# Down projections of a two-layer decoder trunk: seven half-size products for three of four k-tile batches, and a new order of the up and down groups

## The chip, the cores and the metric

The kernel runs on one core of one Trainium2 chip. The metric is the device time of one execution, in microseconds (us), of which the median of several runs is taken. TensorE (PE) multiplies, with its weight loads (PEld) beside it; VectorE (DVE) and ScalarE (ACT) do the elementwise work, GpSimd (POOL) very little of it, and SyncE (SP) issues the loads of the weights.

## What is computed

256 tokens of width 2048 pass through two layers. Each layer adds a mixer (differential attention in the first, an RG-LRU block in the second), a squared-ReLU MLP with 8192 hidden columns, and a gated per-layer embedding:

```python
def sqrelu_mlp(xn, w_up, w_down):
    return jnp.square(jax.nn.relu(xn @ w_up)) @ w_down

    for i in range(DEPTH):                      # DEPTH = 2
        h = h + mix(rmsnorm(h, g_mix[i]))       # attention or RG-LRU
        h = h + sqrelu_mlp(rmsnorm(h, g_mlp[i]), w_up[i], w_down[i])
        ple_gate = jax.nn.sigmoid(rmsnorm(h, g_ple[i]) @ w_ple_gate[i])
        h = h + ple_gate * (p[i] @ w_ple_proj[i])
```

Everything is float32. `w_up` is 2048 x 8192 and `w_down` 8192 x 2048 in each layer.

## The kernel before

All products with weights run through one stream (`stream`). Its unit is a `Group`: 256 tokens by 512 columns of one weight, over `nk` k-tiles of 128 rows. The weights of a group come in chunks of four k-tiles (one load of 1 MB, issued by SyncE at L351, three raw buffers `w_raw`), and each chunk is cut into two `Sub`s of two k-tiles. A sub is split into two float32r parts of 12 significant bits each: ScalarE casts `w_hi` (L255) and VectorE subtracts to get `w_lo` (L256), both 128x1024. Four buffer pairs hold such parts; a sub is split three subs ahead of its products, as far as these buffers allow.

A product of two split operands takes three matmuls per k-tile and token tile (`mm3`, L249 to L251: high by high, low by high, high by low), each of 512 moving columns. One sub of an ordinary group is therefore 2 token tiles x 2 k-tiles x 3 = 12 matmuls. The up projection is computed transposed (`flip`): the weights are the stationary operand and the activations with both parts side by side the moving one, which takes 16 matmuls per sub (L391), 8 of 512 and 8 of 256 columns, on four PSUM accumulators.

The MLP (`mlp`) works in slices of 1024 hidden columns. `up(c)` is two flipped groups over 16 k-tiles, 8 subs each. Their evict (`up_evict`) adds the two halves of each accumulator (ScalarE copy L644, VectorE add L645), takes `relu(.) ** 2` in one VectorE operation (L646) and splits the result into the slice's tiles `big`. `down(c)` is four groups (512 output columns each) over the slice's 8 k-tiles, 4 subs each, and their evict adds the product, scaled by a row factor, to the residual `h` (L589). The slices are emitted as up(0), up(1), down(0), up(2), down(1), and so on, so that two up groups and four down groups alternate.

A scheduler fixes the order of each engine's instructions when the program is built. On the chip each engine then runs its own list in that order, and semaphores make it wait for the others. PSUM has six accumulators `acc` and two tiles `tp`, which serve transposes.

## Time and profile before

| | us |
|---|---|
| median of 3 runs | 2327.42 (2326.64 to 2328.0) |
| profiled execution, span | 2326.8 |
| TensorE busy | 2308.8 (99%) |
| VectorE busy | 1424.6 (61%) |
| ScalarE busy | 1193.6 (51%) |
| the two MLP stages | 707.6 each (403.73 to 1111.34, 1515.47 to 2223.08) |

The span runs from the first to the last instruction of one profiled execution, and lies 0.6 us under the median. Busy time is the union of an engine's instructions. Matmuls are listed with a duration that overlaps the next one, so the pace of TensorE is read from the distance between starts. "Idle before" an instruction is put down to what released it last.

### The profile page before, as it was taken

The numbers are of one execution on the slowest core, as the hardware profiler recorded it, in microseconds if no ns is written. First come the engines' busy times: TensorE is split into PE (matmuls) and PEld (weight loads), VectorE is DVE, ScalarE is ACT, GpSimd is POOL, SyncE is SP. The second block draws the span as 40 slices with busy tenths as digits, with TensorE's granted clock in tenths as the row PEclk, the third lists the DMA queues.
The fourth block names the chain that finished last, engine by engine and source line by source line (L and its number), as shares of the span: only waits on it lengthen the run. The fifth ranks groups of instructions, "written<-read, shape, count | busy, mean of one in ns | idle before, by whom it ended". The sixth has DMA issues, their size and how long they took to land.

```text
span 2326.8 us, 28564 instructions
## 1 busy us (share of the span) xinstructions
PE 2308.8 (99%) x11467; PEld 1946.9 (84%) x11467; DVE 1424.6 (61%) x1704; ACT 1193.6 (51%) x1594; POOL 44.7 (2%) x79
## 2 busy tenths in 40 slices
PE   8999999999999999999999999999999999999999
PEld 6888888888888888888888887888888888888887
DVE  6676655565565665566566767566565555565654
ACT  6555554444444444444558887454444444444453
POOL 2100000000000000000000000000000000000000
PEclk9999999999999999999999999999999999999999
DMA  7454555555565655655566565556565565555554
GB/s 241 163 185 163 165 179 181 185 195 189 191 197 184 198 188 192 196 185 181 189 193 219 187 212 181 181 182 198 184 197 190 191 197 184 198 189 191 177 199 148
DMA packets 225396, 438.95 MB, mean 189 GB/s; under 512 B 7582, under 2 KB 16416, under 8 KB 225264
## 3 DMA queue, kind: packets, MB, share of 16 engines
q1 hardware_dynamic: 224608, 436.24, 57.3%
q8 instruction: 89, 1.46, 0.3%
q0 software_dynamic: 608, 0.89, 0.2%
q14 instruction: 43, 0.35, 0.0%
q10 hardware_dynamic: 48, 0.02, 0.0%
HBM read 435.01 MB, written 2.10 MB: 188 GB/s over the span
## 4 chain that ended last, share of the span: by engine, by line
PE 94%; DVE 2%; ACT 2%; DMA 1%; issue 1%; SPq 0%; POOL 0%; DVEq 0%; ACTq 0%
PE acc L391 31%; PE acc L251 21%; PE acc L249 20%; PE acc L250 20%; PE tp L317 1%; DVE w_lo L256 1%; ACT w_hi L255 1%; DMA w_raw<-in_w_gate_x_dram 0%; DVE t L770 0%; DMA h<-in_x_dram 0%; PE tp L458 0%; DVE big L827 0%; ACT L810 0%; SPq L351 0%; ACT L788 0%
## 5 line engine op out<-in xcount | busy, mean ns | idle before, releaser
L256 DVE TENSOR_TENSOR w_lo<-w_raw,w_hi 128x1024 fp32r<-128x1024 f32 x808 | 987.4, 1224 | 781.4 <-ACT w_hi L255 779.9
L255 ACT CAST w_hi<-w_raw 128x1024 fp32r<-128x1024 f32 x808 | 849.0, 1052 | 979.8 <-PE acc L251 605.7
L391 PE MATMUL acc<-x,w_hi 128*128 128x512 f32 x2048 | 704.8, 394 | 0.0
L391 PE MATMUL acc<-x,w_lo 128*128 128x256 f32 x2048 | 547.8, 278 | 0.0
L249 PE MATMUL acc<-w_hi,x 128*128 128x512 f32 x1152 | 457.1, 397 | 0.0
L250 PE MATMUL acc<-w_lo,x 128*128 128x512 f32 x1152 | 450.2, 391 | 1.9 <-DVE w_lo L256 1.8
L251 PE MATMUL acc<-w_hi,x 128*128 128x512 f32 x1152 | 450.5, 391 | 0.0
L391 PEld LDWEIGHTS acc<-x,w_hi 128*128 128x128 f32 x2048 | 376.0, 188 | 78.6
L249 PE MATMUL acc<-w_hi,big 128*128 128x512 f32 x1024 | 399.7, 390 | 0.0
L251 PE MATMUL acc<-w_hi,big 128*128 128x512 f32 x1024 | 398.6, 389 | 0.0
L250 PE MATMUL acc<-w_lo,big 128*128 128x512 f32 x1024 | 398.4, 389 | 0.0
L391 PEld LDWEIGHTS acc<-x,w_lo 128*128 128x128 f32 x2048 | 384.7, 188 | 11.2
L251 PEld LDWEIGHTS acc<-w_hi,x 128*128 128x128 f32 x1152 | 216.8, 188 | 46.8 <-DVE x L256 0.2
L250 PEld LDWEIGHTS acc<-w_lo,x 128*128 128x128 f32 x1152 | 217.2, 189 | 45.0 <-DVE w_lo L256 3.0
L249 PEld LDWEIGHTS acc<-w_hi,x 128*128 128x128 f32 x1152 | 216.8, 188 | 41.7
L251 PEld LDWEIGHTS acc<-w_hi,big 128*128 128x128 f32 x1024 | 192.2, 188 | 40.3
L250 PEld LDWEIGHTS acc<-w_lo,big 128*128 128x128 f32 x1024 | 192.3, 188 | 39.8
L249 PEld LDWEIGHTS acc<-w_hi,big 128*128 128x128 f32 x1024 | 192.2, 188 | 39.0
L589 DVE SCALAR_TENSOR_TENSOR h<-acc,n_r,h 128x512 f32<-128x512 f32 x128 | 89.9, 744 | 0.0
L644 ACT COPY t<-acc 128x256 f32<-128x256 f32 x128 | 47.5, 371 | 22.8 <-PE acc L391 20.6
L259 ACT ACTIVATE x<-tp,cols_a 128x256 fp32r<-128x256 f32 (+1 forms) x72 | 35.7, 496 | 39.5 <-DVE x L260 39.5
L260 DVE SCALAR_TENSOR_TENSOR x<-tp,cols_a,x 128x256 fp32r<-128x256 f32 (+1 forms) x72 | 36.8, 511 | 18.8 <-ACT x L259 18.8
(173 smaller groups left out, 1064.2 us busy)
## 6 DMA issues: line engine op xcount, KB each, us to landing
w_raw<-in_w_up_dram SPq DMA_DIRECT2D x128, 1024.0 KB, 5.2
w_raw<-in_w_down_dram SPq DMA_DIRECT2D x128, 1024.0 KB, 5.1
w_raw<-in_w_qkv_dram SPq DMA_DIRECT2D x47, 1024.0 KB, 5.2
w_raw<-in_w_ple_gate_dram SPq DMA_DIRECT2D x32, 1024.0 KB, 5.2
w_raw<-in_w_in_rec_dram SPq DMA_DIRECT2D x32, 1024.0 KB, 5.5
w_raw<-in_w_o_attn_dram SPq DMA_DIRECT2D x16, 1024.0 KB, 5.2
w_raw<-in_w_o_rec_dram SPq DMA_DIRECT2D x16, 1024.0 KB, 5.1
w_raw<-in_w_ple_proj_dram SPq DMA_DIRECT2D x8, 512.0 KB, 3.7
```

What stands on the lines that cost most here:

```text
L249: nc.tensor.matmul(ps, lhsT=lh, rhs=rh, start=start, stop=False)
L250: nc.tensor.matmul(ps, lhsT=lh, rhs=rl, start=False, stop=False)
L251: nc.tensor.matmul(ps, lhsT=ll, rhs=rh, start=False, stop=stop)
L255: nc.scalar.copy(hi, src)
L256: nc.vector.tensor_tensor(lo, src, hi.bitcast(F32), op=ALU.subtract)
L259: nc.scalar.activation(hi, src, AF.Copy, scale=scale)
L260: nc.vector.scalar_tensor_tensor(lo, in0=src, scalar=scale, in1=hi.bitcast(F32), op0=ALU.mult, op1=ALU.subtract)
L317: nc.tensor.transpose(tp[:, i, t * P : (t + 1) * P], h[:, t, (k0 + i) * P : (k0 + i + 1) * P], ident)
L391: nc.tensor.matmul(o, lhsT=lh, rhs=rh, start=k == 0 and n == 0, stop=k == g.nk - 1 and n == 1)
L589: nc.vector.scalar_tensor_tensor(hb, in0=acc[t], scalar=scale()[:, t : t + 1], in1=hb, op0=ALU.mult, op1=ALU.add)
L644: nc.scalar.copy(other, ps[:, SEQ:])
```

## The change

The hidden columns of a layer are taken in 16 batches of 4 k-tiles. For three of four batches (those whose number is not a multiple of 4) the down projection is computed on 2 x 2 blocks: token tile by k-tile parity on the left, k-tile parity by 512 output columns on the right. Seven products of such blocks stand in place of eight (`FORMS`), and some of their operands are sums of blocks. The left sums (`S1` to `S4`) are formed in `up_evict`, before the split, so that a hidden tile has eight forms of which seven are used; the right sums (`U1`, `T2`, `T4`, `T3`) are formed on VectorE from the raw weights, each one form ahead of its split (`split_form`).

A `SevenGroup` covers 256 tokens and 1024 output columns (a `half`) over four batches: the three seven batches first, then the plain one. It accumulates in six `acc` tiles and both `tp` tiles. When the products P1, P5, P6 and P7 are complete, `middle` combines them in two `t4` tiles; at the end `evict` adds four accumulators and four combinations to `h`. Per layer the order is up(0), up(1), then the columns 1024 to 2047 of batches 0 and 1 as two plain groups, then seven times two up groups and one `SevenGroup` (half 0 over batches 0 to 3, half 1 over 2 to 5, half 0 over 4 to 7, and so on), and at the end two plain groups over batches 14 and 15. An up group is one batch, 512 hidden columns.

Chunks and split parts of the seven groups may also use one buffer borrowed from `big` and one pair from `v4` (`ring`). `relu(.) ** 2` is now two ScalarE operations (L803, L804). A chunk that appears again within two chunks is no longer loaded again, which concerns the gate weights of the second layer's mixer. Comments and docstrings are gone as well. The core of the diff:

```diff
+X11, X21, X12, X22, S3, S1, S2, S4 = range(8)
+FORMS = (
+    ("W11", X11, "P1"), ("W21", X12, "P2"), ("U1", S1, "P5"), ("T2", S2, "P6"), ("T4", X22, "P4"),
+    ("T3", S3, "P7"), ("W22", S4, "P3"),
+)
+SUMS = {"U1": ("W11", "W12"), "T2": ("U1", "W22"), "T4": ("T2", "W21"), "T3": ("W12", "W22")}
+BT = 4
...
+    def products(self, i, s):
+
+        b, form, nj = self.what[i]
+        x, out = self.hid[b], []
+        if nj is None:
+            _, f, k = FORMS[form]
+            for j in range(2):
+                out.append((k,) + x.form(j, f) + (s.hi[:, j], s.lo[:, j]))
+        else:
+            n, j = nj
+            for t in range(NT):
+                for kk in range(SK):
+                    out.append((self.plain(n)[t],) + x.lhs(2 * j + kk, t) + (s.hi[:, kk], s.lo[:, kk]))
...
-            if not chunks or chunks[-1] is not s.chunk:
+            if not any(c is s.chunk for c in chunks[-2:]):
                 chunks.append(s.chunk)
...
+                turn["raw"] += c.ring
+                if c.ring and turn["raw"] % (W_RAW + 1) == 0:
+                    c.raw = big([P, KC, NB])
+                else:
+                    c.raw = wraw.tile([P, KC, NB], F32, name="w_raw")
...
+        def split_form(s):
+
+            bl = s.blocks
+            src = bl.of(FORMS[s.form][0])
+            nc.scalar.copy(s.hi, src)
+            after = FORMS[s.form + 1][0] if s.form + 1 < len(FORMS) else None
+            if after in SUMS:
+                load_to(cidx[id(bl.chunks[1])])
+                one, two = (bl.of(nm) for nm in SUMS[after])
+                bl.sums[after] = t4([P, SK, NB])
+                nc.vector.tensor_tensor(bl.sums[after], one, two, op=ALU.add)
+            nc.vector.tensor_tensor(s.lo, src, s.hi.bitcast(F32), op=ALU.subtract)
...
+                    turn["split"] += s.chunk.ring
+                    if s.chunk.ring and turn["split"] % (W_SPLIT + 1) == 0:
+                        s.hi, s.lo = (v4([P, SK, NB], F32R) for _ in range(2))
...
+                    for k, lh, ll, rh, rl, first, last in prods:
+                        nc.tensor.matmul(acc[k], lhsT=lh, rhs=rh, start=first, stop=False)
+                        nc.tensor.matmul(acc[k], lhsT=ll, rhs=rh, start=False, stop=False)
+                    for k, lh, ll, rh, rl, first, last in prods:
+                        nc.tensor.matmul(acc[k], lhsT=lh, rhs=rl, start=False, stop=last)
+                    if i == g.mid:
+                        g.middle(acc)
...
-                    nc.vector.scalar_tensor_tensor(u, in0=u, scalar=0.0, in1=u, op0=ALU.max, op1=ALU.mult)
-                    ks = slice(half * 4 + 2 * b, half * 4 + 2 * b + 2)
-                    split(hid[c].hi[:, ks], hid[c].lo[:, ks], u)
+                    nc.scalar.activation(u, u, AF.Relu)
+                    nc.scalar.activation(u, u, AF.Square)
+                    if bt.seven:
+                        nc.vector.tensor_tensor(f[:, S3 : S1 + 1], f[:, X11 : X21 + 1], f[:, X21 : X22 + 1 : 2], op=ALU.subtract)
+                        nc.vector.tensor_tensor(f[:, S2], f[:, S1], f[:, X11], op=ALU.subtract)
+                        nc.vector.tensor_tensor(f[:, S4], f[:, X12], f[:, S2], op=ALU.add)
+                    split(bt.hi[:, j], bt.lo[:, j], f)
...
+            def middle(acc):
+                c1, cb = t4([P, 2, NB]), t4([P, 2, NB])
+                keep["P1"], keep["M"], keep["B"], keep["N"] = c1[:, 0], c1[:, 1], cb[:, 0], cb[:, 1]
+                nc.scalar.copy(keep["P1"], acc["P1"])
+                nc.vector.tensor_tensor(keep["M"], acc["P6"], keep["P1"], op=ALU.add)
+                nc.vector.tensor_tensor(keep["B"], acc["P7"], keep["M"], op=ALU.add)
+                nc.vector.tensor_tensor(keep["M"], acc["P5"], keep["M"], op=ALU.subtract)
+                nc.vector.tensor_tensor(keep["N"], acc["P5"], keep["B"], op=ALU.subtract)
...
-        up(0)
-        for c in range(1, NFC):
-            up(c)
-            down(c - 1)
-        down(NFC - 1)
+        for b in range(0, NBT, 2):
+            up(b)
+            up(b + 1)
+            if b == 0:
+                down_plain(0, 2, None)
+            elif b % 4 == 0:
+                down(1, range(b - 2, b + 2))
+            else:
+                down(0, range(b - 2, b + 2))
+        down_plain(NBT - 2, 2, norm_out)
```

What this does to the engines' lists is seen at three places. The first is VectorE at the end of an up group. Before, the list has the four adds (L645), the two squares (L646) and the splits of the hidden tiles (`big`) among the weight splits (`w_lo`) of the down group that follows:

```order
L645 TENSOR_TENSOR t_8257<-acc,t_8258 128x256
L645 TENSOR_TENSOR t_8257<-acc,t_8261 128x256
L645 TENSOR_TENSOR t_8267<-acc,t_8268 128x256
L646 SCALAR_TENSOR_TENSOR t_8257<-t_8257 128x512
L645 TENSOR_TENSOR t_8267<-acc,t_8271 128x256
L256 TENSOR_TENSOR w_lo<-w_raw,w_hi 128x1024
L256 TENSOR_TENSOR big<-t_8257,big 128x512
L646 SCALAR_TENSOR_TENSOR t_8267<-t_8267 128x512
L256 TENSOR_TENSOR w_lo<-w_raw,w_hi 128x1024
L256 TENSOR_TENSOR big<-t_8267,big 128x512
L256 TENSOR_TENSOR w_lo<-w_raw,w_hi 128x1024 x2
```

Now, at the same place ahead of the first `SevenGroup` (`t_7321` and `t_7335` are the hidden tiles with their forms, `t_7300` is the sum T2, `t_7354` T4, `t_7367` T3, and `v_7365` the low part of T4):

```order
L471 TENSOR_TENSOR w_lo<-t_7300,w_hi 128x1024
L806 TENSOR_TENSOR t_7321<-t_7321 128x256
L807 TENSOR_TENSOR t_7321<-t_7321 128x128
L806 TENSOR_TENSOR t_7335<-t_7335 128x256
L808 TENSOR_TENSOR t_7321<-t_7321 128x128
L807 TENSOR_TENSOR t_7335<-t_7335 128x128
L808 TENSOR_TENSOR t_7335<-t_7335 128x128
L357 TENSOR_TENSOR big<-t_7321,big 128x1024
L357 TENSOR_TENSOR big<-t_7335,big 128x1024
L470 TENSOR_TENSOR t_7354<-t_7300,w_raw 128x1024
L470 TENSOR_TENSOR t_7367<-w_raw 128x1024
L471 TENSOR_TENSOR v_7365<-t_7354,v_7364 128x1024
```

The split of the fourth form stands ahead of the hidden tiles' sums and splits, and the sum T4 for the fifth form behind them; the low parts of the first three forms stand in front of the piece, before the adds L802.

The second place is VectorE inside the groups with `w_down`. Before, four weight splits and two updates of `h` alternate through a whole stretch of four down groups:

```order
L256 TENSOR_TENSOR w_lo<-w_raw,w_hi 128x1024 x2
L589 SCALAR_TENSOR_TENSOR h<-acc,n_r_3441,h 128x512 x2
L256 TENSOR_TENSOR w_lo<-w_raw,w_hi 128x1024 x4
L589 SCALAR_TENSOR_TENSOR h<-acc,n_r_3441,h 128x512 x2
L256 TENSOR_TENSOR w_lo<-w_raw,w_hi 128x1024 x4
```

Now, in the third seven batch of the first `SevenGroup` (`t_7499`, `t_7511`, `t_7525` and `t_7537` are the sums U1, T2, T4 and T3, `v_7549` the low part of T3 and the last split of the batch):

```order
L470 TENSOR_TENSOR t_7499<-w_raw 128x1024
L471 TENSOR_TENSOR w_lo<-w_raw,w_hi 128x1024
L470 TENSOR_TENSOR t_7511<-t_7499,w_raw 128x1024
L471 TENSOR_TENSOR w_lo<-t_7499,w_hi 128x1024
L470 TENSOR_TENSOR t_7525<-t_7511,w_raw 128x1024
L471 TENSOR_TENSOR w_lo<-t_7511,w_hi 128x1024
L470 TENSOR_TENSOR t_7537<-w_raw 128x1024
L471 TENSOR_TENSOR w_lo<-t_7525,w_hi 128x1024
L471 TENSOR_TENSOR w_lo<-w_raw,w_hi 128x1024
L471 TENSOR_TENSOR v_7549<-t_7537,v_7548 128x1024
L357 TENSOR_TENSOR w_lo<-w_raw,w_hi 128x1024 x2
```

Sums of weight blocks now stand between the weight splits, and the updates of `h` have gone to the end of the group. From `big<-t_7321` in the piece above to `v_7549` in this one the list has 29 operations, all of 128x1024.

The third place is TensorE where the seven batches end and the plain batch begins. Before, there is no such place; one down group follows the other with three kinds of rows:

```order
L249 MATMUL acc<-w_hi,big 128x512
L250 MATMUL acc<-w_lo,big 128x512
L251 MATMUL acc<-w_hi,big 128x512
L249 MATMUL acc<-w_hi,big 128x512
L250 MATMUL acc<-w_lo,big 128x512
```

Now, in the first `SevenGroup` (`v_7548` and `v_7549` are the high and the low part of T3 in the third seven batch):

```order
L514 MATMUL acc<-w_hi,big 128x512
L517 MATMUL acc<-w_lo,big 128x512 x2
L514 MATMUL acc<-v_7548,big 128x512
L515 MATMUL acc<-v_7548,big 128x512
L514 MATMUL acc<-v_7548,big 128x512
L515 MATMUL acc<-v_7548,big 128x512
L517 MATMUL tp<-w_lo,big 128x512 x2
L515 MATMUL acc<-w_hi,big 128x512
L514 MATMUL acc<-w_hi,big 128x512
L517 MATMUL acc<-v_7549,big 128x512 x2
L515 MATMUL acc<-w_hi,big 128x512
```

Three matmuls of the plain batch (the first row, and the two in front of `v_7549`) have been moved ahead of the seven batch's last pair; the other 45 stand behind it, and then the next up group.

## Rows read from the trace of the kernel before

**Rows 1.** The page: busy time by engine, and shares of the chain that ended last:

```profile
PE 2308.8 (99%) x11467; PEld 1946.9 (84%) x11467; DVE 1424.6 (61%) x1704; ACT 1193.6 (51%) x1594; POOL 44.7 (2%) x79
...
PE 94%; DVE 2%; ACT 2%; DMA 1%; issue 1%; SPq 0%; POOL 0%; DVEq 0%; ACTq 0%
```

**Rows 2.** Busy time by stretch: two up groups, then four down groups:

```profile
core 0: us, PE busy (x) PEld busy (x) DVE busy (x) ACT busy (x) POOL busy (x), PEclk, DMA share, GB/s
537.34:581.74 44.40, 44.40 (x258) 38.80 (x256) 24.63 (x28) 20.28 (x25) 0.00 (x0) 1.00 0.59 192
581.74:625.26 43.52, 43.52 (x193) 36.04 (x192) 27.16 (x31) 18.29 (x19) 0.00 (x0) 1.00 0.58 192
```

**Rows 3.** Timeline of TensorE, last up matmul and first down matmuls: start, us, instruction:

```profile
581.50 0.40 PE L391 MATMUL acc<-x,w_hi 128*128 128x512 f32 x1
581.74 0.39 PE L249 MATMUL acc<-w_hi,big 128*128 128x512 f32 x1
581.97 0.39 PE L250 MATMUL acc<-w_lo,big 128*128 128x512 f32 x1
582.20 0.39 PE L251 MATMUL acc<-w_hi,big 128*128 128x512 f32 x1
```

**Rows 4.** Waits: who waited for whom, us in total, times, longest:

```profile
DVE w_lo L256 <- ACT w_hi L255: 779.9, 652, 2.4
ACT w_hi L255 <- PE acc L251: 605.7, 383, 3.6
```

**Rows 5.** VectorE's groups by shape: count, busy us, mean ns of one, idle before:

```profile
L256 DVE TENSOR_TENSOR w_lo<-w_raw,w_hi 128x1024 fp32r<-128x1024 f32 x808 | 987.4, 1224 | 781.4 <-ACT w_hi L255 779.9
...
L589 DVE SCALAR_TENSOR_TENSOR h<-acc,n_r,h 128x512 f32<-128x512 f32 x128 | 89.9, 744 | 0.0
...
L587 DVE TENSOR_TENSOR h<-h,acc 128x512 f32<-128x512 f32 x16 | 10.2, 680 | 0.0
...
L445 DVE TENSOR_TENSOR t<-t,q_r 128x1024 f32<-128x1024 f32 x8 | 9.8, 1226 | 14.7 <-POOL q_r L267 14.7
...
L792 DVE TENSOR_TENSOR big<-t,t 128x256 f32<-128x256 f32 x16 | 6.8, 423 | 15.7 <-ACT t L790 15.7
...
L823 DVE TENSOR_TENSOR big<-big 128x1024 f32<-128x1024 f32 x4 | 4.9, 1223 | 0.8 <-ACT big L822 0.8
...
L494 DVE SCALAR_TENSOR_TENSOR t<-t,z 128x128 f32<-128x128 f32 x8 | 2.4, 346 | 0.0
L493 DVE TENSOR_SCALAR t<-t,z 128x128 f32<-128x128 f32 x8 | 1.9, 278 | 0.0
```

**Rows 6.** Timeline of VectorE, two splits back to back and the next operation:

```profile
1286.90 2.36 DVE L256 TENSOR_TENSOR w_lo<-w_raw,w_hi 128x1024 fp32r<-128x1024 f32 x2 [0.91 <-ACT w_hi L255]
1289.18 0.42 DVE L792 TENSOR_TENSOR big<-t,t 128x256 f32<-128x256 f32 x1
```

**Rows 7.** Timeline of ScalarE at the end of the up groups of rows 2:

```profile
581.94 0.37 ACT L644 COPY t<-acc 128x256 f32<-128x256 f32 x1 [0.32 <-PE acc L391]
582.21 1.05 ACT L255 CAST w_hi<-w_raw 128x1024 fp32r<-128x1024 f32 x1
583.15 0.62 ACT L255 CAST big<-t 128x512 fp32r<-128x512 f32 x1
```

**Rows 8.** Timeline of ScalarE, operations of 512 columns back to back:

```profile
1427.72 0.62 ACT L255 CAST x<-t 128x512 fp32r<-128x512 f32 x1 [1.93 <-DVE t L865]
1428.25 0.62 ACT L851 ACTIVATE t<-t 128x512 f32<-128x512 f32 x1
1428.78 1.03 ACT L255 CAST w_hi<-w_raw 128x1024 fp32r<-128x1024 f32 x1
```

**Rows 9.** The page's DMA issues: count, size, median us to landing:

```profile
w_raw<-in_w_down_dram SPq DMA_DIRECT2D x128, 1024.0 KB, 5.1
```

**Rows 10.** Timeline of TensorE, two holes in the second layer's mixer:

```profile
1328.11 0.50 PE L250 MATMUL acc<-w_lo,x 128*128 128x512 f32 x1 [1.07 <-DVE w_lo L256]
...
1428.87 0.50 PE L250 MATMUL acc<-w_lo,x 128*128 128x512 f32 x1 [0.76 <-DVE w_lo L256]
```

**Rows 11.** Timeline of TensorE at the start of the kernel:

```profile
11.31 1.08 PE L317 MATMUL tp<-ident,h 128*128 128x128 f32 x4 [2.43 <-DMA h<-in_x_dram]
...
13.05 0.63 PE L250 MATMUL acc<-w_lo,x 128*128 128x512 f32 x1
13.48 0.63 PE L251 MATMUL acc<-w_hi,x 128*128 128x512 f32 x1
...
16.04 0.63 PE L249 MATMUL acc<-w_hi,x 128*128 128x512 f32 x1
16.46 0.55 PE L250 MATMUL acc<-w_lo,x 128*128 128x512 f32 x1
```

**Rows 12.** Busy time of the first stretches, columns as in rows 2:

```profile
12.00:16.00 4.00, 4.00 (x11) 3.16 (x10) 1.42 (x3) 3.56 (x8) 0.00 (x0) 1.00 1.05 387
```

More of the change, by code (lines that the diff above doesn't have):

```diff
@@ L43 @@
 class Chunk:
+    ring = 0
     def __init__(self, src, nk):
@@ L51 @@
 class Sub:
-    own = None
+    own, blocks, form = None, None, None
     def __init__(self, chunk, k0):
@@ L367, in stream @@
         for g in groups:
-            acc = [psum([P, NB]) for _ in range(4 if g.flip else NT)]
+            seven = isinstance(g, SevenGroup)
+            if seven:
+                acc = {}
+            else:
+                acc = [psum([P, NB]) for _ in range(4 if g.flip else NT)]
             kt = 0
@@ L377, in stream @@
                     continue
-                if g.flip:
+                if seven:
+                    prods = g.products(i, s)
+                    for q in prods:
+                        if q[0] not in acc:
+                            acc[q[0]] = ps_tp.tile([P, NB], F32, name="tp") if q[0] in ("P3", "Z") else psum([P, NB])
+                    for k, lh, ll, rh, rl, first, last in prods:
[5 more added lines that the diff above has]
+                        g.middle(acc)
+                elif g.flip:
                     x = g.lhs()
@@ new lines, in evict, with up, down @@
+                    split(bt.hi[:, j], bt.lo[:, j], f)
+            return evict
+        def up(b):
+            groups.append(Group(a["w_up"][l], 0, KT_D, b * NB, norm_in, up_evict(b), flip=True))
+        def down(half, bs):
+            n0 = half * 2 * NB
+            hs = [slice(n0 + i * NB, n0 + (i + 1) * NB) for i in range(2)]
+            keep = {}
+            def middle(acc):
[6 more added lines that the diff above has]
+                nc.vector.tensor_tensor(keep["N"], acc["P5"], keep["B"], op=ALU.subtract)
+            def evict(acc):
+                r2 = norm_in().r2
+                for t, n, ps, other in ((0, 0, "P2", "P1"), (1, 0, "P4", "B"), (0, 1, "P3", "M"), (1, 1, "Z", "N")):
+                    hb = h[:, t, hs[n]]
+                    for part in (acc[ps], keep[other]):
+                        nc.vector.scalar_tensor_tensor(
+                            hb, in0=part, scalar=r2[:, t : t + 1], in1=hb, op0=ALU.mult, op1=ALU.add
+                        )
+                if half == 0 and bs[-1] == NBT - 1:
+                    for n in range(2):
+                        norm_out().feed(n)
+            order = [b for b in bs if is_seven(b)] + [b for b in bs if not is_seven(b)]
+            groups.append(SevenGroup(a["w_down"][l], [(b, is_seven(b)) for b in order], n0, hid, middle, evict))
```

110 lines of the change are left out of this document (87 added, 23 removed).

## Prediction

> **What bounds the kernel now.** The page's list of engines and its chain come first: TensorE is busy for 2308.8 of 2326.8 us, VectorE for 61% and ScalarE for 51% of the span, and 94% of the chain that ended last is TensorE [rows 1]. Since matmuls overlap in the profile, busy time alone does not say that TensorE runs at its pace, so the second view is the table of two neighbouring stretches of the first layer's MLP [rows 2]: two up groups take 44.40 us and the four down groups behind them 43.52 us for 192 matmuls, which is 0.2267 us each. The timeline shows the same spacing, 0.22 to 0.23 us from start to start, although each matmul is listed with 0.39 us [rows 3]; the price of a matmul is the spacing. TensorE has no hole in either stretch. VectorE has 24.63 of 44.40 and 27.16 of 43.52 us in them, so it has room there, but not endlessly: 16.4 us per down stretch. The third view is the list of waits [rows 4]: ScalarE's casts wait for TensorE (605.7 us in 383 waits behind L251), because all weight slots are full, and VectorE's `w_lo` waits for the cast. The feeders idle on purpose; they are paced by TensorE. So removed matmuls are worth 0.2267 us each only as long as the feeders keep that room.
>
> **What the change removes.** A seven batch issues 42 matmuls of 512 columns (seven products, two k-tiles, three parts) where a plain batch issues 48. There are 7 groups per layer with 3 seven batches each, 42 in all, so 252 matmuls go: 252 x 0.2267 = 57.1 us. A group of three seven batches and a plain one has 174 matmuls, 39.4 us, instead of 43.5. That is the whole gain, and it is had only if nothing makes TensorE wait. The order shows 11217 matmuls against 11469, and nothing else removed from TensorE.
>
> **What it adds to VectorE.** A plain batch costs four splits, so 4 `w_lo` subtractions. A seven batch costs seven splits and four sums of weight blocks, 11 operations of 128x1024. The subtraction takes 1224 ns and a float32 sum of this size, which the kernel already has at L823, 1223 ns [rows 5]. Back to back they start closer than that: two of them fill 2.36 us and the next operation starts 2.28 us after the first [rows 6], so one costs 1.13 to 1.14 us of the queue; I take 1.13. A seven batch is then 11 x 1.13 = 12.4 us of VectorE against 42 x 0.2267 = 9.5 us of TensorE. **Inside the seven batches the bound passes to VectorE.** ScalarE stays below both, 7 casts x 0.94 (the spacing in [rows 7]) = 6.6 us.
>
> Can VectorE work ahead? It has room in the up groups, but not the buffers: weight parts live in four slots plus one pair borrowed from `v4`, and the first piece of the order shows that only the first three forms of a group (and the sum for the fourth) are made before the up group ends. So the group must be followed in time. T0 is the start of its first matmul.
>
> **The start of a group.** The evict of the last up group sits in front of the fifth form in VectorE's queue, and it is now longer: before, `relu(.)**2` was one VectorE operation, now it is two ScalarE operations per tile, three small VectorE sums and a split of 1024 columns instead of 512. Before, the last accumulator's copy started 0.20 us after T0 (581.94 against 581.74), and the next cast 0.27 us later [rows 3, 7]. Now four ScalarE operations of 512 columns follow that cast. The cast occupies 0.94 us; operations of this size start 0.53 us apart and last 0.62 [rows 8]. The first square is done at 0.47 + 0.94 + 2 x 0.53 + 0.62 = 3.1, the second at 3.6. The three sums of the first tile are priced by 128x256 at 0.42 and by the two nearest 128x128 rows at 0.28 and 0.35 [rows 5]; those of the second tile are interleaved. The first tile is ready at about 4.4, its cast (1.05) ends at 5.5 and VectorE's 1024-column work goes on at 5.55. From there to the last split of the third seven batch stand 29 operations of that size without a gap (two of the evict, 27 of the group): 5.55 + 29 x 1.13 + 0.09 = 38.4 us. One ScalarE hop lies inside, the cast of the fifth form, ready at 10.1 against VectorE's own 10.07, so it costs nothing. TensorE meanwhile does four forms (5.4 us), waits until that cast is ready, about 4.6 us, then runs at VectorE's pace.
>
> **The end of a group.** The third piece of the order shows what TensorE still has to do when the last split lands: its own two matmuls and 45 of the 48 of the plain batch, since only three were moved ahead. 47 x 0.2267 = 10.7 us, and with about 0.2 us for the hop the group ends at T0 + 49.3 us. The plain batch's four splits are covered by it (4 x 1.13 and four middle sums at 0.68, the row of L587 [rows 5], about 7 us). The eight updates of `h`, at 0.744 each [rows 5], stand behind the three splits that the next up group needs first; these last TensorE 3 x 2.77 = 8.3 us (44.40/16 per split), the updates 6 us, so they cost nothing.
>
> **The sum.** 49.3 - 43.52 = 5.8 us per group; 14 x 5.8 = 81 us. The first plain group of a layer needs the second batch after 2 x 2.72 us, while the longer evict gives its first half at 6.7 (5.55 + 1.13): 1.2 us twice, 2.4 us. Loads add nothing: a megabyte lands in 5.1 us [rows 9], and by the times above each refill has landed at least 2 us ahead of its reader, in the queue's own order. Gate weights are now loaded once instead of twice, 16 small loads fewer. TensorE's holes near there (1.07 us and 0.76 us [rows 10]) end with VectorE, not with a load, so this is worth 0 to 2 us; I take 0. The profiled span becomes 2326.8 + 81 + 2.4 = 2410.2; the median lies 0.6 above the span, so I predict **2411 us**, 3.6% slower.
>
> The ends of the unknown costs: evict chain +-0.6 us, spacing 1.13 or 1.14 (29 x 0.01 = 0.3 us), hop to TensorE 0 to 0.4 us. That is 48.2 to 50.6 us per group, 2395 to 2429.
>
> **A rule against the trace.** The spacing of [rows 6] is shorter than the duration by 0.09 us. The Trainium skill, "VectorE: DVE Perf Modes", section "The DRAIN you can't avoid", says that the next operation does not start until the pipe is empty. By that rule 29 operations would cost 1.22 each, 2.6 us more per group, and the time would be 2411 + 37 = 2448. The trace does not agree: 2.28 us for two, not 2.45.
>
> **Rivals.** (a) *TensorE stays the bound*, 2327 - 57 = **2270 us**, faster. It needs the 29 operations to keep up; a group costs as much as before when one takes (43.52 - 10.7 - 5.55)/29 = 0.94 us, and the full gain needs (39.4 - 10.7 - 5.55)/29 = 0.80 us. Every row of this size says 1.22 long and 1.13 apart. It could come only if sums that read float32 and write float32 ran faster than those that write float32r, and L823 and L445, both float32, speak against that [rows 5].
>
> (b) *Holes in VectorE's queue.* Casts stand in a fixed order on ScalarE and wait for slots that TensorE frees; TensorE now waits for VectorE, and VectorE for the cast. For it: [rows 4] show how often casts wait for slots. In each group two casts into the borrowed pair stand ahead of casts that are needed sooner; if each delays VectorE by one cast, a group loses 2 x 0.94 us, 26 us in all: **2437 us**. Against it: by the times above VectorE is two to three operations behind these casts.
>
> (c) *TensorE's clock.* The holes of 4.6 us at each group's start are longer than any in this trace. Ahead of the first matmuls of 512 columns it idled 2.43 us, and these stand 0.43 us apart from 13.05 to 16.46 [rows 11], the pace of 1.2 GHz, though the clock column of that stretch reads 1.00 [rows 12]; later the spacing is 0.23 [rows 3]. If a group's first ten matmuls behind the hole ran so, they would cost 2 us, of which most is hidden because TensorE then waits for VectorE anyway: 2411 to **2439 us**. If the low level held to the group's end, 150 matmuls would take 64 us and the time would be near 2760. The Trainium skill, "TensorE: Matmul & The Clock Gate", section "What's actually happening", says that the default state is throttled and that activity releases it; the start of this trace agrees.
>
> **How the numbers follow.** VectorE-bound groups as worked out: 0.74. Holes (b): 0.10. Clock (c): 0.04. VectorE spaced by its full duration: 0.03. TensorE-bound (a): 0.06. In between, near no change: 0.03. The range 2393 to 2450 holds the forecast's own bounds, (b), the cheap end of (c) and the full-duration case; what is left out is (a), the case near no change and the dear end of (c), about 0.11, and some of the forecast's tails. A measurement of this kernel can tell some 0.2% from no change; faster by more 0.06, within 0.03, slower by more 0.91.
>
> **What would show it.** Right: TensorE's hole of 4 to 5 us in every seven group, ended by the cast of a sum, in front of the fifth form; `w_lo` (L471) spaced 2.3 us with a sum (L470) between, without idle time in front; groups of 49 us between up pairs of 44.4; TensorE some 140 us idle in all, 14 x (49.3 - 39.4), put down to VectorE and ScalarE; VectorE busy near 1850 us, since 294 more operations of 1.22 (360 us), longer splits of the hidden values (26), their sums (47) and the new middle sums (38) come in and the squares (44) go out. Wrong: groups near 39 us (a), idle time of VectorE in front of `w_lo` in the second and third batch (b), matmuls 0.43 us apart (c), or a loss outside the two MLP stages.

## The result, and the profile after

The changed kernel takes 2417.97 us (median of 4 runs, 2417.69 to 2418.08) where the kernel before took 2327.71 on the same chip: a ratio of 1.0389, 95% interval 1.0375 to 1.0404. It is slower by 90 us, against a forecast of 84. The profiled span grew from 2326.8 to 2416.1 us.

The page of the changed kernel, busy time by engine and shares of the chain that ended last, to be read beside [rows 1]:

```profile
PE 2305.4 (95%) x11215; PEld 1913.2 (79%) x11215; DVE 1802.1 (75%) x2134; ACT 1393.1 (58%) x1862; POOL 44.7 (2%) x79
...
PE 31%; DVE 6%; ACT 4%; issue 2%; DMA 0%; SPq 0%; ACTq 0%; DVEq 0%
```

The 252 matmuls are gone, yet TensorE's share of the span fell from 99% to 95%, and VectorE's busy time grew by 377.5 us. The chain is followed back over only 43% of the span here, so it can't be set beside the 94% of before, and the stretches have to be read instead. Two stretches of the first layer answer to [rows 2] (the columns are the same), a pair of up groups and the `SevenGroup` behind it, from its first matmul to the next up group's first:

```profile
565.14:609.55 44.41, 44.41 (x257) 38.81 (x256) 29.01 (x32) 21.11 (x28) 0.00 (x0) 1.00 0.61 209
609.55:659.37 49.82, 42.81 (x175) 32.99 (x174) 48.32 (x53) 30.61 (x34) 0.00 (x0) 0.97 0.48 152
```

The up groups take 44.41 us as before. The down groups take 49.82 instead of 43.52; TensorE is busy for 42.81 of them and VectorE for 48.32. All 14 `SevenGroup`s are alike, 49.82 to 50.51 us, 700.56 in all against 14 x 43.52 = 609.3. These 91.3 us are the whole loss: the first plain groups add 0.36 us twice, and everything else together is 2.7 us shorter.

TensorE's timeline at the start of that group (T0 = 609.55; start, us, instruction, and in brackets the idle time before it and what ended it):

```profile
609.32 0.40 PE L533 MATMUL acc<-x,w_hi 128*128 128x512 f32 x1
609.55 0.39 PE L514 MATMUL acc<-w_hi,x 128*128 128x512 f32 x1
...
614.54 0.61 PE L517 MATMUL acc<-w_lo,x 128*128 128x512 f32 x2
619.76 0.79 PE L514 MATMUL acc<-v,x 128*128 128x512 f32 x1 [4.60 <-ACT v L464]
620.35 0.63 PE L515 MATMUL acc<-v,x 128*128 128x512 f32 x1
620.78 0.63 PE L514 MATMUL acc<-v,x 128*128 128x512 f32 x1
```

After four forms TensorE stands still for 4.60 us, until the cast of the fifth form. Behind the hole its matmuls start 0.43 us apart. VectorE's timeline of the same group, from the three small sums of the hidden tiles to the first splits of the plain batch:

```profile
612.67 0.42 DVE L806 TENSOR_TENSOR t<-t 128x256 f32<-128x256 f32 x1 [0.34 <-ACT t L804]
...
614.20 0.29 DVE L808 TENSOR_TENSOR t<-t 128x128 f32<-128x128 f32 x1
615.13 2.36 DVE L357 TENSOR_TENSOR x<-t,x 128x1024 fp32r<-128x1024 f32 x2 [0.64 <-ACT x L356]
617.41 1.22 DVE L470 TENSOR_TENSOR t<-t,w_raw 128x1024 f32<-128x1024 f32 x1
618.54 1.22 DVE L470 TENSOR_TENSOR t<-w_raw 128x1024 f32<-128x1024 f32 x1
619.68 1.22 DVE L470 TENSOR_TENSOR t<-w_raw,big 128x1024 f32<-128x1024 f32 x1
...
645.79 1.22 DVE L471 TENSOR_TENSOR w_lo<-w_raw,w_hi 128x1024 fp32r<-128x1024 f32 x1
646.93 1.22 DVE L471 TENSOR_TENSOR v<-t,v 128x1024 fp32r<-128x1024 f32 x1
648.06 2.35 DVE L357 TENSOR_TENSOR w_lo<-w_raw,w_hi 128x1024 fp32r<-128x1024 f32 x2
```

From 615.13 to 648.15 the 29 operations run with no idle time, 1.13 to 1.14 us from start to start. TensorE's timeline from its last hole in the group to the last split's two matmuls (L517 with `v`), which stand between matmuls of the plain batch, and the busy time from that hole to the group's end (columns of [rows 2]):

```profile
643.68 0.50 PE L514 MATMUL acc<-w_hi,x 128*128 128x512 f32 x1 [0.60 <-ACT w_hi L464]
...
648.15 0.39 PE L515 MATMUL acc<-w_hi,big 128*128 128x512 f32 x1
648.38 0.40 PE L514 MATMUL acc<-w_hi,big 128*128 128x512 f32 x1
648.61 0.62 PE L517 MATMUL acc<-v,x 128*128 128x512 f32 x2
```

```profile
643.68:659.37 15.69, 15.69 (x68) 12.86 (x69) 15.69 (x17) 10.13 (x11) 0.00 (x0) 1.00 0.66 213
```

The last split is done at 648.15, and its matmuls start 0.46 us later, with no hole in front of them: TensorE is busy with other matmuls and does not wait for that split. Its last wait is at 643.68, for the cast of the sum T4 of the third seven batch. VectorE's sum and ScalarE's cast:

```profile
641.25 1.22 DVE L470 TENSOR_TENSOR t<-t,w_raw 128x1024 f32<-128x1024 f32 x1
```

```profile
642.58 1.05 ACT L464 CAST w_hi<-t 128x1024 fp32r<-128x1024 f32 x1 [1.22 <-DVE t L470]
```

That sum is the 24th of the 29 operations. In all 14 groups TensorE's last hole ends with this cast, 15.69 to 15.74 us ahead of the group's end, and 68 matmuls without a hole fill the rest.

The list of waits (who waited for whom, us in total, times, longest) names the same place 14 times, and answers to [rows 4]:

```profile
DVE w_lo L357 <- ACT w_hi L356: 430.0, 385, 2.3
...
PE acc L514 <- ACT v L464: 64.5, 14, 4.6
...
DVE w_lo L471 <- ACT w_hi L464: 32.0, 42, 1.6
...
PE acc L514 <- ACT w_hi L464: 29.8, 47, 0.9
```

In the stretches of [rows 2] TensorE had no hole. Now it waits 64.5 us in the 14 long holes and 29.8 in 47 small ones, while VectorE's waiting for the casts of plain splits, of which there are fewer, fell from 779.9 to 430.0.

### The profile page after: what moved, and what is told of

Same layout as the page of the kernel before. It is cut to its first block, busy times and chain, and to the rows that moved or that the text cites. A ratio compares the mean times of both kernels' runs of the same rounds, so it can differ in the third digit from the quotient of the medians.

```text
span 2416.1 us, 29067 instructions
## 1 busy us (share of the span) xinstructions
PE 2305.4 (95%) x11215; PEld 1913.2 (79%) x11215; DVE 1802.1 (75%) x2134; ACT 1393.1 (58%) x1862; POOL 44.7 (2%) x79
## 5 line engine op out<-in xcount | busy, mean ns | idle before, releaser
L357 DVE TENSOR_TENSOR w_lo<-w_raw,w_hi 128x1024 fp32r<-128x1024 f32 x612 | 742.2, 1222 | 431.3 <-ACT w_hi L356 430.0
L356 ACT CAST w_hi<-w_raw 128x1024 fp32r<-128x1024 f32 x612 | 640.9, 1051 | 605.8 <-PE acc L533 289.2
L350 PE MATMUL acc<-w_hi,x 128*128 128x512 f32 x1216 | 482.7, 397 | 0.0
L351 PE MATMUL acc<-w_lo,x 128*128 128x512 f32 x1216 | 475.1, 391 | 1.7 <-DVE w_lo L357 1.7
L352 PE MATMUL acc<-w_hi,x 128*128 128x512 f32 x1216 | 475.1, 391 | 0.0
L352 PEld LDWEIGHTS acc<-w_hi,x 128*128 128x128 f32 x1216 | 228.6, 188 | 49.7 <-DVE x L357 0.6
L351 PEld LDWEIGHTS acc<-w_lo,x 128*128 128x128 f32 x1216 | 229.1, 188 | 47.1 <-DVE w_lo L357 2.9
L350 PEld LDWEIGHTS acc<-w_hi,x 128*128 128x128 f32 x1216 | 228.7, 188 | 44.7 <-ACT x L356 0.9
L464 ACT CAST w_hi<-t 128x1024 fp32r<-128x1024 f32 x126 | 131.6, 1048 | 151.6 <-DVE t L470 106.8
L471 DVE TENSOR_TENSOR w_lo<-t,w_hi 128x1024 fp32r<-128x1024 f32 x126 | 153.6, 1219 | 28.1 <-ACT w_hi L464 28.0
L464 ACT CAST w_hi<-w_raw 128x1024 fp32r<-128x1024 f32 x98 | 100.0, 1047 | 48.2 <-PE acc L533 46.4
L514 PE MATMUL acc<-w_hi,x 128*128 128x512 f32 x268 | 112.7, 420 | 13.1 <-ACT w_hi L464 13.1
L471 DVE TENSOR_TENSOR w_lo<-w_raw,w_hi 128x1024 fp32r<-128x1024 f32 x98 | 117.1, 1218 | 4.0 <-ACT w_hi L464 4.0
L514 PE MATMUL acc<-w_hi,big 128*128 128x512 f32 x236 | 95.1, 403 | 16.7 <-ACT w_hi L464 16.7
L515 PE MATMUL acc<-w_hi,x 128*128 128x512 f32 x268 | 109.3, 408 | 0.0
L514 PE MATMUL acc<-v,x 128*128 128x512 f32 x68 | 35.4, 521 | 64.5 <-ACT v L464 64.5
L515 PE MATMUL acc<-w_hi,big 128*128 128x512 f32 x236 | 92.3, 391 | 0.0
L517 PE MATMUL acc<-w_lo,x 128*128 128x512 f32 x268 | 85.7, 402 | 0.0
```

The costliest lines, as they stand in the source:

```text
L350: nc.tensor.matmul(ps, lhsT=lh, rhs=rh, start=start, stop=False)
L351: nc.tensor.matmul(ps, lhsT=lh, rhs=rl, start=False, stop=False)
L352: nc.tensor.matmul(ps, lhsT=ll, rhs=rh, start=False, stop=stop)
L356: nc.scalar.copy(hi, src)
L357: nc.vector.tensor_tensor(lo, src, hi.bitcast(F32), op=ALU.subtract)
L464: nc.scalar.copy(s.hi, src)
```

## The experiments

The theory is the prediction's: **VectorE's list, from the end of the evict to the last split of the third seven batch, sets the length of a group, and TensorE's holes only show it.** By the rows above the operation that TensorE waits for last is not that split but a sum five operations ahead of it in the same list. The rivals are that the hole at the group's start is the loss, that TensorE's clock behind the hole is, that the new order of the groups is, and that the casts' order is.

### The sums left out, the order alone, the hole filled

**The weight sums left out.**

```diff
-                bl.sums[after] = t4([P, SK, NB])
-                nc.vector.tensor_tensor(bl.sums[after], one, two, op=ALU.add)
+                bl.sums[after] = two
```

> The four sums of weight blocks per seven batch are left out: a form that needs a sum takes its second block unsummed, so the down projections are no longer what the reference asks for; all splits and matmuls stay. Theory (VectorE's queue is the bound inside the seven groups): 7 x 1.13 = 7.9 us of VectorE per batch lie under 9.5 us of TensorE, so a group falls from 50.0 us to between 39.4 us (matmuls alone) and 43 us (with what is left of the hole at its start): 2270 to 2320 us. Rival (the hole at the group's start and TensorE's lower clock after it are the loss, the sums are not): groups near 49 us, over 2400 us.

Measured: 2278.36 us, ratio 0.9789 [0.9774, 0.9803]. One group of this kernel, columns as in [rows 2]:

```profile
599.56:639.67 40.11, 40.10 (x176) 32.51 (x175) 38.82 (x46) 29.98 (x33) 0.00 (x0) 1.00 0.58 197
```

No hole is left, and the groups are 40.1 us, near the 39.4 of 174 matmuls. With the same products, order, casts and evict, 12 operations fewer per group on VectorE turn a loss of 90 us into a gain of 49. The order of casts, the borrowed buffers and the longer evict alone make no holes.

**The order alone**, no seven batch at all; `down` emits two ordinary groups over its four batches, in buffers of their size (the edit's core):

```diff
-        return b % PERIOD != 0
+        return False
```

> The new order of up and down groups, buffers and two-step relu**2 of the changed kernel, but no seven products: each group of four batches is two plain groups over 16 k-tiles. Theory (the order costs nothing, the loss comes with the seven batches and with the forms of the hidden tiles): 43.5 us per four batches, 2322 to 2332 us. Rival (order, two ScalarE operations for relu**2 or fewer evicts move the time): outside these bounds.

Measured: 2325.19 us, ratio 0.9992 [0.9983, 1.0001]. The new order of the groups and `relu(.) ** 2` in two operations cost nothing where no hidden tile has forms. (Only seven groups borrow buffers, so this run says nothing of those.)

**The hole filled** with matmuls whose result is thrown away (the next matmul on that accumulator starts it anew):

```diff
+                    if i == 4:
+                        k0, lh0, _, rh0, _, _, _ = before
+                        for _ in range(18):
+                            nc.tensor.matmul(acc[prods[0][0]], lhsT=lh0, rhs=rh0, start=True, stop=True)
+                    before = prods[0]
```

> The changed kernel with 18 matmuls (4.1 us) in each of the 14 groups between the fourth and the fifth form; their result is overwritten. They lie in the hole of 4.6 us, so TensorE does not idle in front of the fifth form. Theory: the lower clock behind the hole costs a group only what is not hidden behind VectorE, 0.2 to 0.7 us, so the matmuls of 0.43 us spacing go and the time falls to 2408 to 2416 us. Rival (the clock is most of the loss): below 2395 us.

Measured: 2415.30 us, ratio 1.0379 [1.0363, 1.0394]. Granted clock (the last column but two) in the changed kernel behind the hole:

```profile
619.50:622.00 2.50, 2.24 (x5) 1.49 (x5) 2.50 (x4) 2.36 (x4) 0.00 (x0) 0.50 0.88 259
622.00:626.00 4.00, 4.00 (x17) 3.24 (x17) 4.00 (x5) 2.69 (x3) 0.00 (x0) 0.89 0.44 117
626.00:632.00 6.00, 6.00 (x28) 4.75 (x27) 6.00 (x6) 3.05 (x3) 0.00 (x0) 1.00 0.58 180
```

and the same group with the hole filled:

```profile
609.48:659.32 49.84, 45.96 (x194) 35.40 (x193) 48.35 (x53) 30.73 (x34) 0.00 (x0) 1.00 0.47 152
```

After 4.60 us of idleness TensorE came back at the lower level, 1.2 GHz; the stretch from 626 on is at 2.4 GHz again. With the hole filled the clock stays at 1.00, and the group is as long as in the changed kernel, 49.84 against 49.82. All 14 groups now lie between 49.84 and 49.92, where six of the changed kernel's 14 are 49.98 to 50.51: the slow clock costs 2.7 us in all (2417.97 against 2415.30). The clock is not the loss.

### Work taken off VectorE's list

**The weight sums on GpSimd.**

```diff
-                nc.vector.tensor_tensor(bl.sums[after], one, two, op=ALU.add)
+                nc.gpsimd.tensor_tensor(bl.sums[after], one, two, op=ALU.add)
```

> The four sums of weight blocks per seven batch are made by GpSimd instead of VectorE, nothing else changes. Theory: VectorE is relieved as in the kernel without sums; if GpSimd takes at most 2.4 us per sum (a quarter of a batch's 9.5 us of matmuls) and does not slow VectorE, a group costs 40 to 45 us: 2280 to 2350 us. If a sum takes GpSimd longer, it becomes the bound: four sums of 3 us give 12 us per batch, about what VectorE gives now, 2400 to 2420 us. Rival (VectorE is not the bound): no change from 2418.

Measured: 2592.42 us, ratio 1.1138 [1.1119, 1.1156], worse than every figure of the expectation. GpSimd's and VectorE's groups by shape (count, busy us, mean ns of one, idle before):

```profile
L470 POOL TENSOR_TENSOR t<-t,w_raw 128x1024 f32<-128x1024 f32 x70 | 226.4, 3235 | 152.8 <-DVE big L357 74.0 <-DVE x L357 58.3 <-DVE w_lo L471 17.2
```

```profile
L471 DVE TENSOR_TENSOR w_lo<-t,w_hi 128x1024 fp32r<-128x1024 f32 x126 | 271.9, 2183 | 9.3 <-ACT w_hi L464 8.9
L471 DVE TENSOR_TENSOR w_lo<-w_raw,w_hi 128x1024 fp32r<-128x1024 f32 x98 | 252.4, 2604 | 27.3 <-ACT w_hi L464 27.3
```

A sum takes 3.2 us there, and VectorE's splits beside it take 2.2 and 2.6 us instead of 1.22. The work has left VectorE's list and the list has become longer. The timelines of both engines show that the stretching goes with the overlap, and whom it hits. GpSimd:

```profile
647.97 3.31 POOL L470 TENSOR_TENSOR t<-big 128x1024 f32<-128x1024 f32 x1 [3.43 <-DVE v L471]
651.25 3.38 POOL L470 TENSOR_TENSOR t<-w_raw 128x1024 f32<-128x1024 f32 x1
```

VectorE at the same time (asked for in short windows, so that each operation has a row):

```profile
646.68 1.21 DVE L471 TENSOR_TENSOR v<-t,v 128x1024 fp32r<-128x1024 f32 x1
647.82 1.21 DVE L471 TENSOR_TENSOR w_lo<-t,w_hi 128x1024 fp32r<-128x1024 f32 x1
648.95 3.42 DVE L471 TENSOR_TENSOR w_lo<-t,w_hi 128x1024 fp32r<-128x1024 f32 x1
652.29 3.42 DVE L471 TENSOR_TENSOR v<-w_raw,v 128x1024 fp32r<-128x1024 f32 x1
```

At 646.68 GpSimd is idle and the split takes 1.21 us. The split at 647.82 starts 0.15 us ahead of a sum, overlaps with it and still takes 1.21; the next, at 648.95, starts while the sum runs, takes 3.42 and ends 1.09 us behind it. So it is over the whole trace: all 61 of VectorE's subtractions of this size that began ahead of a sum that overlaps with them took 1.21 to 1.23 us, the 154 that began while one ran 1.80 to 3.46. GpSimd's sums took 2.35 to 2.41 us where no such subtraction ran at their start, and 2.42 to 3.39 where one did. The Trainium skill, "SBUF — State Buffer", section "SBUF: two separate sides", says that VectorE operations with two SBUF inputs and GpSimd operations that read SBUF take turns on one shared pair of ports. The trace agrees, and it speaks for turns: with a shared bandwidth the operation that starts first would be stretched as well, and it is not.

**`relu(.) ** 2` back on VectorE**, one operation per tile in place of two on ScalarE:

```diff
-                    nc.scalar.activation(u, u, AF.Relu)
-                    nc.scalar.activation(u, u, AF.Square)
+                    nc.vector.scalar_tensor_tensor(u, in0=u, scalar=0.0, in1=u, op0=ALU.max, op1=ALU.mult)
```

> The changed kernel with relu**2 as one VectorE operation, as before the change, instead of two ScalarE operations. Theory: the evict in front of T4 is shorter by some 1.1 us (two operations of 0.6 us on VectorE that lie in its idle time replace four of 0.53 us on ScalarE in the chain), 2400 to 2410 us. Rival (VectorE's load alone counts): 64 operations more make it slower, up to 2430 us.

Measured: 2408.28 us, ratio 1.0349 [1.0334, 1.0364]. The chain ahead of the hidden tiles is shorter, the hole falls from 4.6 to 2.7 us with a second one, mostly near 1.2, behind it, and the groups are 49.4 us in the mean instead of 50.0. That is 0.65 us per group and not the 1.1 of the theory: the split of the fourth form, which ran in VectorE's idle time ahead of the hidden tiles' sums (T0 + 1.56), now stands among them (T0 + 3.50).

**The raw form first**: the last form, which needs no sum, stands fifth, so that its split goes ahead of the evict in VectorE's list.

```diff
-    ("W11", X11, "P1"), ("W21", X12, "P2"), ("U1", S1, "P5"), ("T2", S2, "P6"), ("T4", X22, "P4"),
-    ("T3", S3, "P7"), ("W22", S4, "P3"),
+    ("W11", X11, "P1"), ("W21", X12, "P2"), ("U1", S1, "P5"), ("T2", S2, "P6"), ("W22", S4, "P3"),
+    ("T4", X22, "P4"), ("T3", S3, "P7"),
```

> The changed kernel with the last form of a seven batch, whose right block is a raw weight block and needs no sum, moved to the fifth place. Its split can then stand ahead of the evict in VectorE's list. Theory (VectorE's list from the end of the evict to the last split sets the group): the list behind the evict has 28 operations instead of 29, the hole falls from 4.6 to about 3.2 us, and each group is 1.13 us shorter, 2418 - 16 = about 2402 us (2394 to 2410). Rival (the hole itself is the loss, and its slack is lost elsewhere only in part): the hole vanishes and the groups are 4 us shorter, 2350 to 2370.

Measured: 2409.22 us, ratio 1.0353 [1.0337, 1.0368]. The hole falls to 3.3 to 3.6 us as expected, the groups by 0.6 us, about half of the 1.13 expected. TensorE's last wait in a group (T0 = 608.87) shows why:

```profile
645.26 0.50 PE L514 MATMUL acc<-w_hi,x 128*128 128x512 f32 x1 [1.24 <-ACT w_hi L464]
```

It now ends with the cast of T3, the last form, at T0 + 36.39. The sum T3 is the 26th operation of VectorE's list behind the evict, where the sum that TensorE waited for last before (T4) was the 24th; behind the wait stand 56 matmuls instead of 68. Two operations more (2.26 us) and 12 matmuls fewer (2.79 us) make this group 49.30 us instead of 49.82. So an operation less in the list did not bring the group's end forward by an operation, because TensorE waits for a sum ahead of the list's end; and the group did not follow the hole either, which shrank by 1.1 to 1.3 us per group, 15 to 19 us in all where 8.8 were measured.

### How many seven batches, and where they stand

**One seven batch of four** (number 2 of each four), the others plain; two branches more, left out here, give the plain batches buffers of their size:

```diff
-        return b % PERIOD != 0
+        return b % PERIOD in (2,)
```

> One of four batches in seven products (number 2 modulo 4), three plain. Theory and the rival of the hole alone are close here: 42.2 us of matmuls and the 4.6 us hole give 46.8 us, VectorE's chain 47.2 us, so 2373 to 2380 us. If holes came from the number of seven batches alone (no loss at the group's start), a group would cost 42.2 to 43.5 us: 2310 to 2327 us.

**Two of four** (numbers 2 and 3), the same edit with `(2, 3)`:

> Two of four batches in seven products (numbers 2 and 3 modulo 4), two plain; order of groups as in the changed kernel. Theory: start of the chain 5.6, 18 operations of 1.135 on VectorE, then 95 matmuls behind the last split: 5.6 + 20.5 + 22 = 48.1 us per group, 2391 us. Rival (the hole at the start is the whole loss, VectorE keeps up otherwise): 40.8 us of matmuls + 4.6 us = 45.4 us, 2353 us.

Measured: one of four 2310.68 us, ratio 0.9928 [0.9914, 0.9943], 0.7% faster than before; two of four 2347.47 us, ratio 1.0087 [1.0072, 1.0102]. Neither is what the theory gave: the first lies at the lower end of its rival's 2310 to 2327, the second near its rival's 2353. One group of the kernel with one seven batch:

```profile
601.04:643.52 42.48, 42.48 (x187) 34.89 (x186) 29.38 (x32) 22.59 (x27) 0.00 (x0) 1.00 0.45 154
```

and two neighbouring groups of the kernel with two:

```profile
608.18:649.98 41.80, 41.44 (x181) 33.69 (x180) 37.69 (x42) 25.35 (x30) 0.00 (x0) 1.00 0.60 195
694.38:742.15 47.77, 42.67 (x182) 33.29 (x180) 41.88 (x48) 27.02 (x30) 0.00 (x0) 1.00 0.53 177
```

In the second kernel the groups alternate, with the same products in each: eight of 46.66 to 48.90 us, six of 41.65 to 43.40. The long ones are near the theory's 48.1; the rival's 45.4 is near the mean of the two kinds, but no group has it. The long one stands behind the up group of batch 3, a seven batch whose evict makes forms; the short one behind that of batch 1 (modulo 4), a plain batch. I had charged every group with the long evict, though it comes only where **the batch in front of the group** is a seven batch; in the kernel with one seven batch that is never so. So the theory was used wrongly: it holds for a group behind an evict that makes forms. The evict alone is not enough, since without the sums, in the first run, it makes forms ahead of every group and the groups are 40.1 us. The next run tests this.

**Even batches seven, odd ones plain**, two of four, and always a plain batch in front of the group (the buffers, left out here, are given to match):

```diff
-        return b % PERIOD != 0
+        return b % 2 == 0
```

> Two of four batches in seven products, the even ones, so that the up group right in front of each down group is a plain batch, whose evict has no forms. Theory after the kernel with batches 2 and 3: its groups behind a plain batch took 41.7 us, those behind a seven batch 47.7; here all 14 are of the first kind, 14 x (41.7 - 43.5) = -25 us from before: 2298 to 2308 us. Rival (the two lengths there came from the half of the columns or from the batches' order): groups of 41.7 and 47.7 again, near 2347 us.

Measured: 2316.51 us, ratio 0.9952 [0.9935, 0.9968], 8.5 us over the upper end of the expectation. No long group is left: the 14 take 42.20 to 45.26 us, so the rival, groups of 41.7 and 47.7 again, falls. But they are 43.1 in the mean and not 41.7. TensorE's holes in one group (T0 = 688.71), and the busy time of that stretch (columns of [rows 2]):

```profile
702.50 0.50 PE L514 MATMUL acc<-v,x 128*128 128x512 f32 x1 [0.36 <-ACT v L464]
704.79 0.50 PE L514 MATMUL acc<-w_hi,x 128*128 128x512 f32 x1 [0.64 <-ACT w_hi L464]
707.04 0.73 PE L517 MATMUL acc<-w_lo,x 128*128 128x512 f32 x2 [0.57 <-DVE w_lo L471]
```

```profile
702.00:708.00 6.00, 4.42 (x17) 2.92 (x17) 6.00 (x6) 4.70 (x6) 0.00 (x0) 1.00 0.84 288
```

They lie 13 to 19 us into the group, in the second seven batch (one group of the 14 has another, 1.14 us near its start). VectorE has no idle time in this stretch, so it does not wait for casts there; it is late. No evict with forms stands in front; two seven batches in a row are 2 x 2.9 us dearer on VectorE than on TensorE, and the lead of three forms covers one. How much is left over depends on where VectorE's list stands: the short groups of the kernel with batches 2 and 3 also have two in a row, but the last split of their seven batches is done at T0 + 19.6 in the group shown, here at T0 + 21.7, and four of the six such groups have one hole of 0.3 to 0.4 us. If two deficits in a row make the holes, a plain batch between them must close the holes.

**Even batches seven, in their natural order**: the kernel just shown with one line changed, so that a group runs seven, plain, seven, plain.

```diff
-            order = [b for b in bs if is_seven(b)] + [b for b in bs if not is_seven(b)]
+            order = list(bs)
```

> Batches 0 and 2 of four are seven batches and 1 and 3 plain, as in the run with even batches, but within a group they now stand in their natural order, seven, plain, seven, plain, instead of both seven batches first. Theory (each seven batch costs VectorE 12.4 us against 9.5 us of TensorE, a lead of three forms absorbs one such deficit of 2.9 us but not two in a row, and a plain batch, 4.5 us of VectorE against 10.9, gives the lead back): the holes of 1 to 3 us per group vanish, groups are 180 x 0.2267 = 40.8 to 41.3 us instead of 42.2 to 45.3, and the time is 2317 - 14 x 2 = about 2289 us (2284 to 2297). Rival (the holes come from the fixed order of casts and borrowed buffers, not from two deficits in a row): the time stays at 2310 to 2320.

Measured: 2291.79 us, ratio 0.9850 [0.9834, 0.9866]: 1.5% faster than the kernel before. Its groups, columns as in [rows 2]:

```profile
599.55:640.63 41.08, 41.08 (x181) 33.77 (x180) 38.38 (x40) 25.77 (x30) 0.00 (x0) 1.00 0.60 199
685.03:726.21 41.18, 41.18 (x182) 33.76 (x180) 37.67 (x40) 25.88 (x30) 0.00 (x0) 1.00 0.64 222
```

TensorE has no hole, with VectorE busy for 38 of 41 us as in the kernel with the sevens together, whose group above had 37.66 of 43.62. The same work in another order, with the same evict; VectorE's three waits for casts at the group's start are the same too (0.64, 0.16 and 0.24 us there, 0.63, 0.16 and 0.25 in the second group here). So the holes came from two deficits in a row.

**The plain batch second**, the changed kernel with three seven batches and one thing moved:

```diff
-            order = [b for b in bs if is_seven(b)] + [b for b in bs if not is_seven(b)]
+            order = [b for b in bs if is_seven(b)]
+            order.insert(1, [b for b in bs if not is_seven(b)][0])
```

> The changed kernel with one thing moved: in each group the plain batch stands second, behind the first seven batch, instead of last. Theory (the group's length is VectorE's queue to the last split plus what TensorE has left behind it, 10.7 us of the plain batch): the 33 operations up to the last split now end at 5.55 + 33 x 1.13 = 42.8 us, and TensorE has only two matmuls left, so groups are 43.3 to 44 us up to the last matmul; the sums in the middle and the updates of h now stand at the start of the next up group and cost 0 to 3 us there. The time is about 2355 us (2330 to 2385). Rival (the total of VectorE's work sets the group, wherever the plain batch stands): 2405 to 2425.

Measured: 2382.03 us, ratio 1.0238 [1.0222, 1.0253]. The direction is the theory's (36 us less than the changed kernel), the point, 2355, was missed by 27. A group and the up pair behind it:

```profile
606.15:652.98 46.83, 42.22 (x175) 34.19 (x174) 44.95 (x48) 31.37 (x34) 0.00 (x0) 0.93 0.46 157
652.98:698.00 45.02, 45.02 (x257) 39.00 (x256) 34.91 (x43) 21.92 (x28) 0.00 (x0) 1.00 0.62 211
```

Its only hole is the first:

```profile
616.36 0.80 PE L514 MATMUL acc<-v,x 128*128 128x512 f32 x1 [4.61 <-ACT v L464]
```

Behind it TensorE never waits again, and the last split is done 3 us ahead of the group's end (649.96 against 652.98). So the bound has changed sides: 39.4 us of matmuls, 4.6 of hole and about 2.2 for some ten matmuls at the lower clock are 46.2 of the 46.8. I had let VectorE's list set the group without adding up TensorE's own sum. Here the hole and the clock cost in full; in the changed kernel both are hidden under VectorE's longer list.

## Why the prediction was right

**The mechanism held up to the last split of the list.** VectorE goes on with 1024-column work at T0 + 5.58 (predicted 5.55). The last split of the 29 is done at T0 + 38.8 in the mean of the 14 groups (predicted 38.4), and the group ends 11.2 us later (predicted 10.9), at 50.0 instead of 49.3.

**The end of the group is not reached as predicted.** The prediction lets TensorE wait for the last split and then do 47 matmuls. By the rows above it does not wait for it: its last wait is for the cast of the third batch's T4, and 68 matmuls follow. With the prediction's own numbers that path gives 5.55 + 24 x 1.13 + 0.09 for the sum, 1.05 for the cast and 68 x 0.2267 for the matmuls, 49.2 us, within 0.1 us of the path that it named. So the wrong step cost the forecast nothing; but nothing in the prediction makes the two paths equally long, and that they are is luck. The run with the raw form first, whose expectation went by the last split, paid for it: 0.6 us per group instead of 1.13.

**The sizes that were off** are 0.74 us per group, 10 us of the time, counted along the prediction's path:

- 0.37 on the list. The spacing was 1.135, not 1.13 (0.15 us in 29 operations); six groups have 0.04 to 0.59 us of idle time in front of one split, ended by a cast. This is rival (b) in a small dose: with the hole filled and the clock at 1.00 all groups are 49.84 to 49.92 long, so it comes with the slow matmuls that free the cast's slot later.
- 0.34 at the end. The 0.46 us from the last split to its first matmul (648.15 to 648.61) are no hop of 0.2, since TensorE is busy in them, and the 47 matmuls stand 0.229 us apart.
- 0.03 at the chain's start.

Against that stand errors the other way: the first plain groups lost 0.36 us each, not 1.2, and the rest of the kernel gained 2.7 us where I had put 0 (the first MLP stage begins at 402.84 us instead of 403.73, and the stretch between the two MLP stages, in which the gate weights are loaded once, takes 402.0 us instead of 404.1). 2326.8 + 91.3 + 0.7 - 2.7 = 2416.1.

**Busy times.** VectorE's is 1802 us, not 1850. I counted new operations at their full duration, but back to back each fills 1.135 us of the union and not 1.22; over some 33 operations in a row in each group that is 14 x 33 x 0.085 = 39 us, most of the difference. TensorE's idle time is 110.7 us, not 140, since a matmul's listed duration reaches into the hole and the slow ones count as busy.

**Loads** cost nothing, as predicted, though not for the reason given: one load did not land in time. The first sum of a group waited for it nine times, 10.4 us in all:

```profile
L470 DVE TENSOR_TENSOR t<-w_raw 128x1024 f32<-128x1024 f32 x56 | 68.2, 1218 | 10.4 <-DMA w_raw<-in_w_down_dram 10.4
```

All nine waits lie 7 to 8 us ahead of a group, while the up group still runs and VectorE has room.

**The rivals.** (a) TensorE as the bound: it needed 0.80 us per operation; 1.135 was measured. The run without sums shows that its time, 2270, was the right price for a VectorE that keeps up (2278). (b) was there with 0 to 0.6 us per group, in six groups, instead of 1.9. (c) was there: 0.43 us between matmuls at a granted clock of 0.50. It cost 2.7 us, since VectorE was behind anyway; the order with the plain batch second shows its full price, about 2.2 us in the group shown. The price by the rule on the pipe fell: 1.135 from start to start, not 1.22. The Trainium skill, "VectorE: DVE Perf Modes", section "The DRAIN you can't avoid", says in the same paragraph that a next operation that is not held starts earlier; the prediction left that half out, and the trace agrees with it.

## What to carry to other kernels

An algorithm that trades matmuls for elementwise sums has to be priced on the engine that makes the sums, stage by stage and in the order of its list; the share of busy time over the whole kernel (61% before) said that there was room for it. Where one stretch costs the feeder more than the consumer, what counts is the buffers' lead and what stands between such stretches: the same two seven batches per group cost 2316.5 us in a row and 2291.8 with a plain batch between them. A long hole in the fast engine may be hidden entirely under another engine's list, so look for what is late at the stretch's end before filling it.

## What was not expected of the hardware

GpSimd and VectorE hold each other up: of a float32 sum of 128x1024 on GpSimd and a subtraction of that size on VectorE, both with two SBUF operands, the one that started first kept its time (2.35 to 2.41 and 1.21 to 1.23 us), and the other waited, up to 3.39 and 3.46 us in all. And an idle time of 4.6 us was enough for TensorE to come back at the lower of its two levels, though it had been at 1.00 all through the up group before. With the raw form first the holes are 3.3 to 3.6 us, and two of the 14 groups stay at 1.00 behind them while the others fall.
